# A hybrid decoder block on one core: the split weights of the MLP, the output projection and the branches stand at other places in their buffers from block to block

## Chip, cores and metric

The kernel runs on one core of a Trainium2 chip. The metric is the device time of one execution in microseconds, given as the median of several runs. Lower is better.

## What is computed

The reference is one decoder layer on 256 tokens of width 2048 with 16 learned tokens ahead of them (272 positions). Two mixers run side by side on the normalized input, RWKV-7 and a forgetting attention, are gated and merged, and a SwiGLU MLP of width 5632 follows.

```
proj = rms(h, n1) @ w_in                          # 2048 x 10704
y_a, y_b = rwkv7(...), fox(...)                   # 1024 wide each
g_a, g_b = split(sigmoid(z_gate))
merged = g_a * (y_a @ w_a) + g_b * (y_b @ w_b)    # "branches"
h = h + merged @ w_o                              # "output projection"
gate, up = split(rms(h, n2) @ w_gu)               # MLP, 2 x 5632 columns
return h + (silu(gate) * up) @ w_dn
```

All of it is float32.

## The kernel before

Every large matrix product is done in split precision. A weight block of 128 x 1024 words is loaded by one DMA into a tile `raw` (four buffers). ScalarE (ACT) copies it, rounded, into a tile `wh` (the high part), and VectorE (DVE) writes the remainder `raw - wh` into a tile `wl` (the low part); there are four buffers of each, and a buffer has 1088 words in each partition. The helper `wload` (L304) issues these three steps. Activations are split likewise into a high and a low part that lie next to each other, 272 words each, so the pair of one block of 128 features takes 544 words in each partition. Of the four products of parts three are taken.

Three kinds of block use these weights.

- *MLP, gate and up* (`cm_jobs`, L432, called at L1369 and L1370): 11 blocks of each, named `gt0` to `gt10` and `up0` to `up10`, with 512 columns of the weight each. The weights are the stationary operand (128 x 128), the activation tile `hts` moves. `mm2` (L419) gives one matmul of 512 columns with `wh`, which moves the high and the low part of the activation one after the other (L423), and one of 256 columns with `wl`, which moves the high part (L425; L422 in the last feature block). A block is 16 feature blocks by 4 column groups: 64 such pairs, fed by 8 loads.
- *Branches* (`cm_jobs` from `branch_jobs`, L1259): 16 blocks of 256 weight columns, fed by 2 loads each. `mm3` (L346) gives three matmuls of 256 columns: `wh` with the high part (L347), `wh` with the low part (L348), `wl` with the high part (L349). There are 16 such triples in a block.
- *Output projection and down projection* (`tm_jobs`, L1285; called at L1329 for `wo0` to `wo3` and L1378 for `dn0` to `dn3`): here the activations (`mgh`, `mgl`, `ach`, `acl`) are stationary, and the weights move, 512 columns at a time, as two stretches of 256 words that stand 272 words apart. Three matmuls to a triple: L1304 (high weights, high activation), L1305 (high weights, low activation) and L1306 (low weights, high activation). 32 triples in a `wo` block, 88 in a `dn` block.

In `cm_jobs` the split weights fill the first 1024 words of their buffer, one feature block behind the other, from word 0 on. In `tm_jobs` (`gap=True`) the four stretches of 256 words begin at words 16, 288, 560 and 832:

```
th, tl = (t.rearrange("p (r c) -> p r c", c=L)[:, :, NMETA:] for t in (wh, wl))
```

The order of the work on TensorE (PE) is the program's own. A load is issued ahead of the matmuls of the block that came before it (`run`, L408), so that loading and splitting run beside the matmuls. The gate columns of `w_in` (`zg`), and other columns of `w_in`, use `cm_jobs` as well. All the blocks named above come after the first 613 us of the execution, in the order branches, output projection, gate and up, down projection.

Of the kernel before, what the change touches and what calls it, by code (L numbers as in the profile page):

```python
# [18 lines left out]
P = 128  # L19
D = 2048  # L20
NMETA = 16

T = 256
L = NMETA + T
# [3 lines left out]
DFF = 5632  # L28
# [6 lines left out]
KT = D // P  # L35
# [18 lines left out]
GATEB = 3  # L54
PSM = 4
WCOLS = 4 * L

LANES = 112
BETWEEN = 2
# [41 lines left out]
def hybrid_block(ctx, tc, A, out, dbg=None):  # L101
# [199 lines left out]
        nc.tensor.matmul(pz, zw, zw, start=True, stop=True)  # L301


    def wload(parts, n, between=None, gap=False):  # L304

        raw = wp.tile([P, 1024], F32, tag="raw", name="raw", bufs=RAWB)
        wh = wp.tile([P, WCOLS], F32R, tag="wh", name="wh", bufs=WB)
        wl = wp.tile([P, WCOLS], F32R, tag="wl", name="wl", bufs=WB)  # L310
        if gap:

            (_, _, shape, ((_, src),)), = parts
            nc.sync.dma_start(raw.rearrange("p (k c) -> p k c", c=shape[1]), src)
            rr = raw.rearrange("p (r c) -> p r c", c=T)
            th, tl = (t.rearrange("p (r c) -> p r c", c=L)[:, :, NMETA:] for t in (wh, wl))
            nc.scalar.activation(th, rr, AF.Copy)  # L317
            nc.vector.tensor_tensor(tl, rr, th.bitcast(F32), op=ALU.subtract)  # L318
            return [(th, tl)]
        res = []  # L320
        for prow, c0, shape, srcs in parts:
            size = 1
            for d in shape:
                size *= d
            names = " ".join(f"d{i}" for i in range(len(shape)))
            kw = {f"d{i}": d for i, d in enumerate(shape)}

            def v(t):
                return t[:prow, c0:c0 + size].rearrange(f"p ({names}) -> p {names}", **kw)

            for sel, src in srcs:
                nc.sync.dma_start(v(raw)[sel], src)
            if between is not None:
                between(len(res))
            cs_ = slice(c0, c0 + size)
            nc.scalar.activation(wh[:prow, cs_], raw[:prow, cs_], AF.Copy)  # L336
            nc.vector.tensor_tensor(wl[:prow, cs_], raw[:prow, cs_], wh[:prow, cs_].bitcast(F32), op=ALU.subtract)  # L337
            res.append((v(wh), v(wl)))
        return res
# [3 lines left out]
    def kblock(ap):  # L343
        return ap.rearrange("(k p) c -> p k c", p=P)
# [63 lines left out]
    def run(jobs):  # L408
        for load, mul in jobs:
            w = load()  # L410
            finish_job()
            pending.append(lambda w=w, mul=mul: mul(w))
# [16 lines left out]
        nc.scalar.activation(dst, ps[:, :T], AF.Copy)  # L429
        nc.vector.tensor_tensor(dst, dst, ps[:, T:], op=ALU.add)  # L430

    def cm_jobs(wap, nk, act, n0, n, post, alloc=main_ps, name="cm", two=True):  # L432


        box = []
        cols = wap.shape[1]
        nm, kb = cols // P, 1024 // cols

        def mk(q):
            def load():  # L440
                return wload([(P, 0, [kb, cols], [((ALL,), kblock(wap[q * kb * P:(q + 1) * kb * P, :]))])], 1024)

            def mul(w):
                (wh, wl), = w
                if q == 0:
                    box.extend(alloc(f"{name}_{m}") for m in range(nm))
                for m in range(nm):
                    ms = slice(m * P, (m + 1) * P)
                    for k in range(kb):
                        kt = q * kb + k  # L450
                        a = act[:, kt, :, n0:n0 + n]
                        if n == T and two:
                            mm2(box[m], wh[:, k, ms], wl[:, k, ms], a, kt == 0, kt == nk - 1)
                        else:
                            mm3(box[m][:, :n], wh[:, k, ms], wl[:, k, ms], a[:, 0], a[:, 1], kt == 0, kt == nk - 1)
                        slot(3 * n / 2.4)
                if q == nk // kb - 1:
                    post(box)
            return load, mul
        return [mk(q) for q in range(nk // kb)]  # L460
# [778 lines left out]
    def branch_jobs(j):  # L1239
        tl = gate_tile(j)  # L1240
        for b in range(2):
            if (j, b) in spilled:
                nc.sync.dma_start(tl[:, b], zgd[j, :, b])
        jobs = []

        def post(b):
            def f(pss):
                if b == 0:
                    tf = tl.rearrange("p b m t -> p (b m) t")
                    nc.vector.tensor_tensor(tf, tf, bcast(rsb[:, NMETA:], 4), op=ALU.mult)  # L1250
                    nc.scalar.activation(tl, tl, AF.Sigmoid)
                for m in range(2):
                    nc.vector.tensor_tensor(tl[:, b, m, :], pss[m][:, :T], tl[:, b, m, :], op=ALU.mult)
                if b == 1:
                    nc.vector.tensor_tensor(tl[:, 0], tl[:, 0], tl[:, 1], op=ALU.add)
                    split(mgh[:, 2 * j:2 * j + 2, :], mgl[:, 2 * j:2 * j + 2, :], tl[:, 0])
            return f
        for b, (wn, act) in enumerate((("w_branch_a", yas), ("w_branch_b", ybs))):
            jobs += cm_jobs(A[wn][0][:, j * 256:(j + 1) * 256], 8, act, NMETA, T, post(b),  # L1259
                            alloc=aux_ps, name=f"br{b}{j}", two=False)  # L1260
        return jobs

    ahead = gate_jobs()
# [18 lines left out]
    rs2 = hp.tile([P, 2], F32, tag="rs2", name="rs2")  # L1282
    rsb2 = hp.tile([P, T], F32, tag="rsb2", name="rsb2")

    def tm_jobs(wap, nk, ah, al, post, name):  # L1285

        box = []

        def mk(q):
            def load():  # L1290
                return wload([(P, 0, [2, 512], [((ALL,), kblock(wap[q * 256:(q + 1) * 256, :]))])], 1024, gap=True)

            def mul(w):
                (wh, wl), = w
                if q == 0:
                    box.extend(main_ps(f"{name}_{t}") for t in range(2))
                end = q == nk // 2 - 1
                for k, t in ((0, 0), (1, 0), (0, 1), (1, 1)):
                    kt = q * 2 + k
                    ts_ = slice(t * P, (t + 1) * P)  # L1300
                    first, last = kt == 0, kt == nk - 1
                    o = box[t].rearrange("p (a c) -> p a c", a=2)
                    hi, lo_ = wh[:, 2 * k:2 * k + 2], wl[:, 2 * k:2 * k + 2]
                    nc.tensor.matmul(o, ah[:, kt, ts_], hi, start=first, stop=False)  # L1304
                    nc.tensor.matmul(o, al[:, kt, ts_], hi, start=False, stop=False)  # L1305
                    nc.tensor.matmul(o, ah[:, kt, ts_], lo_, start=False, stop=last)  # L1306
                    if end and k == 1:
                        post(t, box[t])
            return load, mul
        return [mk(q) for q in range(nk // 2)]  # L1310

    for j in range(4):
        js = slice(j * 512, (j + 1) * 512)
        nc.sync.dma_start(hh[:, :, js], x[:, js].rearrange("(t p) c -> p t c", p=P))

        def post(t, ps, j=j, js=js):
            nc.vector.tensor_tensor(hh[:, t, js], ps, hh[:, t, js], op=ALU.add)
            jk = hp.tile([P, 512], F32, tag="jk", name=f"jk{j}{t}", bufs=2)
            nc.scalar.activation(jk, hh[:, t, js], AF.Square, accum_out=ss2[:, t, j:j + 1])
            if t == 0:  # L1320
                return
            for k in range(4 * j, 4 * j + 4):
                pt = aux_ps(f"hT{k}")[:, :T]
                for t in range(2):
                    nc.tensor.transpose(pt[:, t * P:(t + 1) * P], hh[:, t, k * P:(k + 1) * P], ident)
                tmp = hp.tile([P, T], F32, tag="htmp", name=f"htmp{k}", bufs=3)
                nc.vector.tensor_scalar(tmp, pt, vc("n2", k), None, op0=ALU.mult)
                split(hts[:, k, 0, NMETA:], hts[:, k, 1, NMETA:], tmp)
        run(tm_jobs(A["w_o"][0][:, js], KT, mgh, mgl, post, f"wo{j}"))  # L1329
    finish_job()  # L1330
    nc.vector.tensor_reduce(rs2, ss2, axis=AX.X, op=ALU.add)
    ms2 = hp.tile([P, 2], F32, tag="ms2", name="ms2")
# [20 lines left out]
    for j in range(DFF // 512):  # L1353
# [8 lines left out]
        def post_up(pss, gs=gs, j=j):  # L1362
            for m, (g, ps) in enumerate(zip(gs, pss)):
# [2 lines left out]
                nc.vector.tensor_tensor(ub, ub, rsb2, op=ALU.mult)  # L1366
                nc.vector.tensor_tensor(ub, ub, g, op=ALU.mult)
                split(ach[:, 4 * j + m, :], acl[:, 4 * j + m, :], ub)
        run(cm_jobs(wgu[:, j * 512:(j + 1) * 512], KT, hts, NMETA, T, post_gate, name=f"gt{j}"))  # L1369
        run(cm_jobs(wgu[:, DFF + j * 512:DFF + (j + 1) * 512], KT, hts, NMETA, T, post_up, alloc=aux_ps, name=f"up{j}"))  # L1370
    wdn = A["w_down"][0]
    for j in range(4):
        js = slice(j * 512, (j + 1) * 512)

        def post(t, ps, js=js):
            nc.vector.tensor_tensor(hh[:, t, js], ps, hh[:, t, js], op=ALU.add)
            nc.sync.dma_start(out[0][t * P:(t + 1) * P, js], hh[:, t, js])
        run(tm_jobs(wdn[:, js], NF, ach, acl, post, f"dn{j}"))  # L1378
    finish_job()
    hp_pool.__exit__(None, None, None)  # L1380
    ap_pool.__exit__(None, None, None)
# [61 lines left out]
```

## Time and profile before

| | us |
|---|---|
| median of 3 runs | 1537.64 (1537.41 to 1539.07) |
| the profiled execution | 1540.85 |
| its span, first to last instruction | 1539.1 |
| PE busy in the span | 1529.6 (99%) |
| weight loads of PE (PEld) busy | 1352.5 (88%) |
| DVE busy | 1030.4 (67%) |
| ACT busy | 778.2 (51%) |

The page lists, for each engine, the time in which it had an instruction under way. Matmuls overlap: a matmul's listed duration is longer than the time that it holds the array, since the next one starts before it ends. What a matmul costs the kernel is therefore read from the distance between starts. The granted TensorE clock is 0.999 of full speed over the span.

### The profile page before, as it was taken

The numbers are of one execution on the slowest core, as the hardware profiler recorded it, in microseconds if no ns is written. First come the engines' busy times: TensorE is split into PE (matmuls) and PEld (weight loads), VectorE is DVE, ScalarE is ACT, GpSimd is POOL, SyncE is SP. The second block draws the span as 40 slices with busy tenths as digits, with TensorE's granted clock in tenths as the row PEclk, the third lists the DMA queues.
The fourth block names the chain that finished last, engine by engine and source line by source line (L and its number), as shares of the span: only waits on it lengthen the run. The fifth ranks groups of instructions, "written<-read, shape, count | busy, mean of one in ns | idle before, by whom it ended". The sixth has DMA issues, their size and how long they took to land.

```text
span 1539.1 us, 25987 instructions
## 1 busy us (share of the span) xinstructions
PE 1529.6 (99%) x10113; PEld 1352.5 (88%) x10113; DVE 1030.4 (67%) x1859; ACT 778.2 (51%) x1174; POOL 106.8 (7%) x186
## 2 busy tenths in 40 slices
PE   9999999999999999999999999999999999999998
PEld 9999899989989888998888888888888888888887
DVE  7887698688788857876565566666556666444443
ACT  7654465475465445554455455445445544333332
POOL 2111203302202000000000000000000000000000
PEclk9999999999999999999999999999999999999999
DMA  8566546546645757777566666666666665566663
GB/s 269 163 171 185 148 134 188 163 119 188 175 125 154 212 155 218 230 226 240 181 180 185 192 185 186 191 192 182 189 191 191 182 190 189 191 204 204 189 203 104
DMA packets 211483, 283.32 MB, mean 184 GB/s; under 512 B 23888, under 2 KB 128352, under 8 KB 211360
## 3 DMA queue, kind: packets, MB, share of 16 engines
q1 hardware_dynamic: 206752, 277.53, 60.7%
q10 hardware_dynamic: 4608, 4.13, 0.8%
q8 instruction: 79, 1.29, 0.3%
q14 instruction: 44, 0.36, 0.1%
HBM read 274.43 MB, written 7.19 MB: 183 GB/s over the span
## 4 chain that ended last, share of the span: by engine, by line
PE 95%; DVE 2%; ACT 1%; DMA 1%; SPq 1%; issue 1%; DVEq 0%; ACTq 0%
PE up L423 11%; PE gt L423 10%; PE zg L423 8%; PE dn L1306 5%; PE dn L1305 5%; PE dn L1304 5%; PE up L425 5%; PE gt L425 5%; PE zg L425 4%; PE f L347 2%; PE f L349 2%; PE f L348 2%; PE br L347 2%; PE f L423 2%; PE br L348 2%; PE br L349 2%
## 5 line engine op out<-in xcount | busy, mean ns | idle before, releaser
L337 DVE TENSOR_TENSOR wl<-raw,wh 128x1024 fp32r<-128x1024 f32 (+1 forms) x376 | 456.7, 1216 | 264.0 <-ACT wh L336 263.4
L336 ACT ACTIVATE wh<-raw 128x1024 fp32r<-128x1024 f32 (+1 forms) x376 | 393.9, 1049 | 424.8 <-PE up L423 117.5
L318 DVE TENSOR_TENSOR wl<-raw,wh 128x1024 fp32r<-128x1024 f32 x120 | 147.0, 1225 | 162.8 <-ACT wh L317 162.7
L423 PE MATMUL gt<-hts,wh 128*128 128x512 f32 x704 | 245.0, 394 | 0.0
L423 PE MATMUL up<-hts,wh 128*128 128x512 f32 x704 | 244.9, 394 | 0.0
L317 ACT ACTIVATE wh<-raw 128x1024 fp32r<-128x1024 f32 x120 | 127.0, 1058 | 194.4 <-PE dn L1305 141.5
L425 PE MATMUL gt<-hts,wl 128*128 128x256 f32 x660 | 186.2, 282 | 0.0
L425 PE MATMUL up<-hts,wl 128*128 128x256 f32 x660 | 186.0, 282 | 0.0
L423 PE MATMUL zg<-xhl,wh 128*128 128x512 f32 x512 | 182.4, 401 | 0.0
L423 PEld LDWEIGHTS up<-hts,wh 128*128 128x128 f32 x704 | 130.1, 188 | 26.5
L423 PEld LDWEIGHTS gt<-hts,wh 128*128 128x128 f32 x704 | 130.1, 188 | 26.5
L1305 PE MATMUL dn<-wh,acl 128*128 128x512 f32 x352 | 138.7, 394 | 0.0
L1306 PE MATMUL dn<-wl,ach 128*128 128x512 f32 x352 | 138.3, 393 | 0.0
L1304 PE MATMUL dn<-wh,ach 128*128 128x512 f32 x352 | 138.1, 392 | 0.0
L425 PE MATMUL zg<-xhl,wl 128*128 128x256 f32 x480 | 135.0, 281 | 0.0
L425 PEld LDWEIGHTS up<-hts,wl 128*128 128x128 f32 x660 | 124.7, 189 | 1.8
L425 PEld LDWEIGHTS gt<-hts,wl 128*128 128x128 f32 x660 | 124.7, 189 | 1.8
L423 PEld LDWEIGHTS zg<-xhl,wh 128*128 128x128 f32 x512 | 94.3, 188 | 19.4 <-issue 0.7
L425 PEld LDWEIGHTS zg<-xhl,wl 128*128 128x128 f32 x480 | 90.6, 189 | 1.2
L1304 PEld LDWEIGHTS dn<-wh,ach 128*128 128x128 f32 x352 | 66.0, 188 | 15.7
L1305 PEld LDWEIGHTS dn<-wh,acl 128*128 128x128 f32 x352 | 66.1, 188 | 15.4
L1306 PEld LDWEIGHTS dn<-wl,ach 128*128 128x128 f32 x352 | 66.1, 188 | 14.7
(464 smaller groups left out, 2937.9 us busy)
## 6 DMA issues: line engine op xcount, KB each, us to landing
raw<-in_w_gate_up_dram SPq DMA_DIRECT2D x176, 512.0 KB, 3.7
raw<-in_w_in_dram SPq DMA_DIRECT2D x160, 512.0 KB, 4.1
raw<-in_w_down_dram SPq DMA_DIRECT2D x88, 512.0 KB, 4.8
raw<-in_w_o_dram SPq DMA_DIRECT2D x32, 512.0 KB, 4.1
raw<-in_w_branch_a_dram SPq DMA_DIRECT2D x16, 512.0 KB, 4.6
raw<-in_w_branch_b_dram SPq DMA_DIRECT2D x16, 512.0 KB, 4.7
zgd<-zg ACTq DMA_DIRECT2D x30, 128.0 KB, 1.7
gate<-zgd SPq DMA_DIRECT2D x15, 256.0 KB, 6.0
```

The lines of the kernel that those rows point to most:

```text
L317: nc.scalar.activation(th, rr, AF.Copy)
L318: nc.vector.tensor_tensor(tl, rr, th.bitcast(F32), op=ALU.subtract)
L336: nc.scalar.activation(wh[:prow, cs_], raw[:prow, cs_], AF.Copy)
L337: nc.vector.tensor_tensor(wl[:prow, cs_], raw[:prow, cs_], wh[:prow, cs_].bitcast(F32), op=ALU.subtract)
L347: nc.tensor.matmul(ps, wh, ah, start=first, stop=False)
L348: nc.tensor.matmul(ps, wh, al, start=False, stop=False)
L349: nc.tensor.matmul(ps, wl, ah, start=False, stop=last)
L423: nc.tensor.matmul(ps.rearrange("p (a t) -> p a t", a=2), wh, act, start=first, stop=last)
L425: nc.tensor.matmul(ps[:, :T], wl, act[:, 0, :], start=False, stop=False)
L1304: nc.tensor.matmul(o, ah[:, kt, ts_], hi, start=first, stop=False)
L1305: nc.tensor.matmul(o, al[:, kt, ts_], hi, start=False, stop=False)
L1306: nc.tensor.matmul(o, ah[:, kt, ts_], lo_, start=False, stop=last)
```

## The change

Nothing is taken out of the work and nothing is added. `wload` gets a parameter `lay` in place of `gap`, and places its two output tiles by it. Three tables give the places: `PLACES` for the 22 blocks of gate and up, `PLACES_T` for the four blocks of the output projection and the four of the down projection, `PLACES_BR` for the 16 branch blocks. An entry of `PLACES` or `PLACES_BR` is (odd, first word of `wh`, first word of `wl`).

- odd = 0: the 1024 words begin at the given word (0, 8, 16 or 24) in place of word 0.
- odd = 1: even feature blocks stand in the first 544 words of the buffer and odd ones in the second 544, each from the given word on (0 to 32), so that an odd feature block is 544 words behind the even one in place of 512.
- `tm_jobs` has pairs: the four stretches of 256 words begin 0, 8 or 16 words into their 272, for high and low part apart, where it was 16 for both.

`cm_jobs` without an entry (the columns of `w_in`) takes (0, 0, 0). For blocks of 256 columns the four feature blocks of a load now lie in the order 0, 2, 1, 3, so there ScalarE and VectorE read `raw` as four stretches of 256 words. The list of instructions of the built program, with its waits, is the same as before on each engine, but for the shape of the split's output in blocks with odd = 1, which is 128x2x512 in place of 128x1024.

```diff
+PLACES = [(0, a, b) for a in (0, 8, 16, 24) for b in (0, 8, 16, 24)][1:] + [
+    (1, 24, 24), (1, 8, 8), (1, 16, 16), (1, 8, 24), (1, 24, 8), (1, 16, 0), (1, 0, 16)]
+PLACES_T = [(8, 0), (0, 8), (16, 8), (8, 16), (0, 0), (8, 8), (16, 0), (0, 16)]
+PLACES_BR = [(0, 8, 8), (0, 16, 16), (0, 24, 24), (0, 0, 8), (0, 0, 16), (0, 0, 24), (0, 8, 0), (0, 16, 0),
+             (1, 0, 0), (1, 8, 8), (1, 16, 16), (1, 24, 24), (1, 32, 0), (1, 32, 8), (1, 32, 16), (1, 32, 24)]
...
-    def wload(parts, n, between=None, gap=False):
+    def wload(parts, n, between=None, lay=None):
...
-        if gap:
+        if lay is not None:
             (_, _, shape, ((_, src),)), = parts
+            odd, *first = lay
             nc.sync.dma_start(raw.rearrange("p (k c) -> p k c", c=shape[1]), src)
-            rr = raw.rearrange("p (r c) -> p r c", c=T)
-            th, tl = (t.rearrange("p (r c) -> p r c", c=L)[:, :, NMETA:] for t in (wh, wl))
+            if odd is None:
+                rr = raw.rearrange("p (r c) -> p r c", c=T)
+                th, tl = (t.rearrange("p (r c) -> p r c", c=L)[:, :, s:s + T] for t, s in zip((wh, wl), first))
+            else:
+                rr = raw.rearrange("p (j q c) -> p q j c", q=2, c=shape[1])
+                th, tl = ((t if odd else t[:, s:s + 1024]).rearrange("p (q e) -> p q e", q=2)
+                          [:, :, odd and s:(odd and s) + 512].rearrange("p q (j c) -> p q j c", c=shape[1])
+                          for t, s in zip((wh, wl), first))
             nc.scalar.activation(th, rr, AF.Copy)
             nc.vector.tensor_tensor(tl, rr, th.bitcast(F32), op=ALU.subtract)
...
-                            mm2(box[m], wh[:, k, ms], wl[:, k, ms], a, kt == 0, kt == nk - 1)
+                            mm2(box[m], wh[:, k % 2, k // 2, ms], wl[:, k % 2, k // 2, ms], a, kt == 0, kt == nk - 1)
...
-                            alloc=aux_ps, name=f"br{b}{j}", two=False)
+                            alloc=aux_ps, name=f"br{b}{j}", two=False, lay=PLACES_BR[2 * j + b])
...
-        run(tm_jobs(A["w_o"][0][:, js], KT, mgh, mgl, post, f"wo{j}"))
+        run(tm_jobs(A["w_o"][0][:, js], KT, mgh, mgl, post, f"wo{j}", PLACES_T[j]))
...
-        run(cm_jobs(wgu[:, j * 512:(j + 1) * 512], KT, hts, NMETA, T, post_gate, name=f"gt{j}"))
-        run(cm_jobs(wgu[:, DFF + j * 512:DFF + (j + 1) * 512], KT, hts, NMETA, T, post_up, alloc=aux_ps, name=f"up{j}"))
+        run(cm_jobs(wgu[:, j * 512:(j + 1) * 512], KT, hts, NMETA, T, post_gate, name=f"gt{j}",
+                    lay=PLACES[j]))
+        run(cm_jobs(wgu[:, DFF + j * 512:DFF + (j + 1) * 512], KT, hts, NMETA, T, post_up, alloc=aux_ps, name=f"up{j}",
+                    lay=PLACES[11 + j]))
...
-        run(tm_jobs(wdn[:, js], NF, ach, acl, post, f"dn{j}"))
+        run(tm_jobs(wdn[:, js], NF, ach, acl, post, f"dn{j}", PLACES_T[4 + j]))
```

## Rows read from the trace of the kernel before

**Rows 1.** Busy time by stretch: us, then each engine's busy time, clock, DMA, GB/s.
```profile
0.00:620.00 620.00, 614.47 (x5108) 562.28 (x5109) 497.17 (x1156) 354.14 (x628) 106.77 (x186) 1.00 0.60 173
620.00:713.00 93.00, 93.00 (x752) 91.51 (x751) 68.56 (x88) 46.83 (x49) 0.00 (x0) 1.00 0.69 218
713.00:803.00 90.00, 90.00 (x414) 73.11 (x413) 54.60 (x72) 43.78 (x63) 0.00 (x0) 1.00 0.66 206
803.00:1291.00 488.00, 487.87 (x2789) 427.65 (x2788) 295.89 (x438) 241.41 (x345) 0.00 (x0) 1.00 0.65 188
1291.00:1539.00 248.00, 244.22 (x1057) 197.99 (x1055) 114.17 (x108) 92.00 (x91) 0.00 (x0) 1.00 0.57 183
```

**Rows 2.** The page's chain that ended last: share of the span by engine.
```profile
PE 95%; DVE 2%; ACT 1%; DMA 1%; SPq 1%; issue 1%; DVEq 0%; ACTq 0%
```

**Rows 3.** Timeline of PE around the start of `up5` and of `gt6`: start, duration, what.
```profile
1044.61 0.39 PE L423 MATMUL up<-hts,wh 128*128 128x512 f32 x1
1044.84 0.28 PE L425 MATMUL up<-hts,wl 128*128 128x256 f32 x1
1044.95 0.40 PE L423 MATMUL up<-hts,wh 128*128 128x512 f32 x1
...
1067.01 0.39 PE L423 MATMUL gt<-hts,wh 128*128 128x512 f32 x1
```

**Rows 4.** PE groups by line: count, busy time, mean duration of one.
```profile
L423 PE MATMUL gt<-hts,wh 128*128 128x512 f32 x704 | 245.0, 394 | 0.0
L425 PE MATMUL gt<-hts,wl 128*128 128x256 f32 x660 | 186.2, 282 | 0.0
L1305 PE MATMUL dn<-wh,acl 128*128 128x512 f32 x352 | 138.7, 394 | 0.0
L1306 PE MATMUL dn<-wl,ach 128*128 128x512 f32 x352 | 138.3, 393 | 0.0
L1304 PE MATMUL dn<-wh,ach 128*128 128x512 f32 x352 | 138.1, 392 | 0.0
```

**Rows 5.** Tile `up`, 1050 to 1060 us: durations, minimum/median/maximum, in ns.
```profile
L425 PE MATMUL up<-hts,wl x30: 281/282/283, 1049.7 to 1059.9; 128*128 128x256 f32 x30
L423 PE MATMUL up<-hts,wh x29: 393/396/396, 1049.9 to 1059.7; 128*128 128x512 f32 x29
```

**Rows 6.** Tile `br`, whole span: durations as above.
```profile
L347 PE MATMUL br<-yas,wh x128: 279/282/285, 613.7 to 699.0; 128*128 128x256 f32 x128
...
L349 PE MATMUL br<-yas,wl x128: 280/280/281, 614.0 to 699.2; 128*128 128x256 f32 x128
L347 PE MATMUL br<-ybs,wh x128: 282/284/285, 619.4 to 704.7; 128*128 128x256 f32 x128
...
L348 PE MATMUL br<-ybs,wh x128: 279/280/282, 619.5 to 704.8; 128*128 128x256 f32 x128
```

**Rows 7.** Tile `dn`, 1352 to 1413 us (block `dn1`): durations as above.
```profile
L1306 PE MATMUL dn<-wl,ach x89: 392/394/394, 1351.8 to 1412.8; 128*128 128x512 f32 x89
L1304 PE MATMUL dn<-wh,ach x88: 392/392/393, 1352.0 to 1412.3; 128*128 128x512 f32 x88
...
L1305 PE MATMUL dn<-wh,acl x88: 392/394/396, 1352.3 to 1412.6; 128*128 128x512 f32 x88
```

**Rows 8.** The page's groups of the splits: busy, mean ns | idle before, releaser.
```profile
L337 DVE TENSOR_TENSOR wl<-raw,wh 128x1024 fp32r<-128x1024 f32 (+1 forms) x376 | 456.7, 1216 | 264.0 <-ACT wh L336 263.4
L336 ACT ACTIVATE wh<-raw 128x1024 fp32r<-128x1024 f32 (+1 forms) x376 | 393.9, 1049 | 424.8 <-PE up L423 117.5
L318 DVE TENSOR_TENSOR wl<-raw,wh 128x1024 fp32r<-128x1024 f32 x120 | 147.0, 1225 | 162.8 <-ACT wh L317 162.7
...
L317 ACT ACTIVATE wh<-raw 128x1024 fp32r<-128x1024 f32 x120 | 127.0, 1058 | 194.4 <-PE dn L1305 141.5
```

**Rows 9.** Chain that ended last, 803 to 900 us: start, us, what.
```profile
803.39 1.07 ACT wh L336
804.48 1.23 DVE wl L337
```

**Rows 10.** PE groups by line: the output projection and one branch line.
```profile
L1306 PE MATMUL wo<-wl,mgh 128*128 128x512 f32 x128 | 50.6, 396 | 0.0
L1305 PE MATMUL wo<-wh,mgl 128*128 128x512 f32 x128 | 50.6, 395 | 0.0
L1304 PE MATMUL wo<-wh,mgh 128*128 128x512 f32 x128 | 50.3, 393 | 0.0
...
L347 PE MATMUL br<-ybs,wh 128*128 128x256 f32 x128 | 36.3, 284 | 0.0
L347 PE MATMUL br<-yas,wh 128*128 128x256 f32 x128 | 36.3, 283 | 0.0
```

More of the change, by code (lines that the diff above doesn't have):

```diff
@@ L430, in halves, with cm_jobs @@
         nc.vector.tensor_tensor(dst, dst, ps[:, T:], op=ALU.add)
-    def cm_jobs(wap, nk, act, n0, n, post, alloc=main_ps, name="cm", two=True):
+    def cm_jobs(wap, nk, act, n0, n, post, alloc=main_ps, name="cm", two=True, lay=(0, 0, 0)):
         box = []
@@ L440, in load @@
             def load():
-                return wload([(P, 0, [kb, cols], [((ALL,), kblock(wap[q * kb * P:(q + 1) * kb * P, :]))])], 1024)
+                return wload([(P, 0, [kb, cols], [((ALL,), kblock(wap[q * kb * P:(q + 1) * kb * P, :]))])], 1024,
+                             lay=lay)
             def mul(w):
@@ L452, in mul @@
                         if n == T and two:
-                            mm2(box[m], wh[:, k, ms], wl[:, k, ms], a, kt == 0, kt == nk - 1)
+                            mm2(box[m], wh[:, k % 2, k // 2, ms], wl[:, k % 2, k // 2, ms], a, kt == 0, kt == nk - 1)
                         else:
-                            mm3(box[m][:, :n], wh[:, k, ms], wl[:, k, ms], a[:, 0], a[:, 1], kt == 0, kt == nk - 1)
+                            mm3(box[m][:, :n], wh[:, k % 2, k // 2, ms], wl[:, k % 2, k // 2, ms], a[:, 0], a[:, 1],
+                                kt == 0, kt == nk - 1)
                         slot(3 * n / 2.4)
@@ L1283, in hybrid_block, with tm_jobs @@
     rsb2 = hp.tile([P, T], F32, tag="rsb2", name="rsb2")
-    def tm_jobs(wap, nk, ah, al, post, name):
+    def tm_jobs(wap, nk, ah, al, post, name, lay=(NMETA, NMETA)):
         box = []
@@ L1290, in load @@
             def load():
-                return wload([(P, 0, [2, 512], [((ALL,), kblock(wap[q * 256:(q + 1) * 256, :]))])], 1024, gap=True)
+                return wload([(P, 0, [2, 512], [((ALL,), kblock(wap[q * 256:(q + 1) * 256, :]))])], 1024,
+                             lay=(None, *lay))
             def mul(w):
```

## The prediction

> **What bounds the kernel now.** I read the stretches first. From 620 us on, PE is busy without a break: 93.00 of 93.00 us in the branches, 90.00 of 90.00 in the output projection, 487.87 of 488.00 in gate and up, at a granted clock of 1.00, which is the 2.4 GHz level [rows 1]. DVE has 295.89 us of work in the 488 and ACT 241.41, so both splitting engines rest four tenths of the time or more. The chain of work that ended last says the same: 95% of it lies on PE [rows 2]. So only what a matmul takes counts, and then how long one holds the array. A busy engine does not say that; the distance between starts does.
>
> Block `up5` starts at 1044.61 us and `gt6` at 1067.01 [rows 3]. That is 22.40 us for 64 pairs, 350.0 ns to a pair of 512 and 256 columns. At 2.4 GHz 768 columns would take 320 ns. So about 30 ns of each pair, over 8%, is something other than columns. Within a pair, the 512 columns hold the array for about 0.23 us and the 256 for about 0.11 to 0.12 [rows 3]. Their mean durations are 394 and 282 ns, together 676 [rows 4]; against 350 that leaves 163 ns for each matmul that overlaps the next. I therefore read a duration less 163 ns as the time held: 231 for the 512, 119 for the 256.
>
> This gives a fine scale, for durations are listed to the nanosecond, and they are not all equal. In ten microseconds of `up` the 512-column matmuls take 393 or 396 ns, the 256-column ones 281 to 283 [rows 5]. In the branches the same kind takes 279 to 285 [rows 6]. In `dn1` L1304 takes 392 or 393 and L1305 392 to 396 [rows 7]. Column count, engine clock and instruction are the same within each row. What changes from one matmul to the next within a line is the address: the activation pair of the next feature block stands 544 words further on, the weights 512 words or, in the down projection, 544. So I take it that **the place of the operands matters, by up to about 6 ns in 119 and 4 in 231**. Which relation of the two places is good the rows do not say.
>
> **The change, part by part.** Loads, splits and matmuls keep their number and their order, so nothing is removed or added on any queue, and no wait is new. Three things remain.
>
> *The splits.* ACT and DVE write shifted or two-part outputs, and in blocks of 256 columns they read four stretches. The nearest row is the split that already writes four stretches of 256 words: 1058 ns on ACT and 1225 on DVE, against 1049 and 1216 for the plain one (a mean that has a few smaller ones in it) [rows 8]. So about 9 ns on each. In gate and up a load's 8 pairs hold PE for 2.8 us, and one split costs DVE 1.23 and ACT 1.07: hidden, and it stays so until a split grows by a microsecond. ACT waits for PE there to free a buffer (117.5 us behind `up` L423), not PE for ACT [rows 8]. Where the cover is gone, as at the first load of the MLP, one split of each kind stands on the chain [rows 9], and the price is 18 ns at a place; a dozen such places make 0.2 us. If all 160 loads of `w_in` stood bare it would be 160 x 18 ns = 2.9 us, but PE is busy 614.47 of the first 620 us [rows 1]. I take 0.
>
> *The columns of `w_in`* get their feature blocks in another order, moved by 256 words. The `up` rows, where weight blocks are 128, 512 and 1088 words apart in four buffers, show only the two alternating values, 393 and 396, so such steps do not show. I take 0.
>
> *The places in 5024 matmuls.* 22 blocks x 64 = 1408 pairs in gate and up, 480 triples in the output and down projections (1440 matmuls), 256 triples in the branches (768).
>
> The trace of before does not show the new places, so I bound them by the shortest and longest durations of a matmul of that width at the places that it does show: 392 and 396 for 512 columns [rows 7], 279 and 285 for 256 [rows 6].
>
> - Gate and up now 394 + 282 = 676 [rows 4]. All at the short ends: 671, -5 ns x 1408 = -7.0 us. All at the long ends: 681, +7.0 us.
> - Projections: 1056 at (392 + 394 + 393)/3 = 393.0 [rows 4] and 384 at (393 + 395 + 396)/3 = 394.7 [rows 10], mean 393.4. Short -1.4 x 1440 = -2.0 us, long +2.6 x 1440 = +3.7 us.
> - Branches: L347 at 283 and 284 [rows 10], the other two lines at 280 [rows 6], mean 281.2. Short -2.2 x 768 = -1.7 us, long +3.8 x 768 = +2.9 us.
>
> Together -10.7 to +13.6 us, if every new place were the best or the worst of those seen. The tables spread over many places, so an average over relations is the nearer guess. I take for each kind the mean of its own value and that of the other kind of the same width. For 512 columns that is between 394 and 393.4, for 256 between 282 and 281.2. Gate and up: (-0.3 - 0.4) x 1408 = -1.0 us. Projections: +0.3 x 1440 = +0.4. Branches: +0.4 x 768 = +0.3. **Sum: -0.3 us.**
>
> The profiled execution took 1540.85 us with a span of 1539.1, 3.2 us above the median of the runs. A difference of blocks carries over to the median as it is: 1537.64 - 0.3 = 1537.3 us. About 0.2% or 3.1 us is what a measurement of this kernel can tell from no change. Over 5024 matmuls that is **0.61 ns each**, so a small shift of the mean already decides.
>
> **The rivals.**
>
> *Some places make the stall go away.* Of a pair's 350 ns, 30 are not columns [rows 3]. If a place had nothing of that, a block of 64 pairs would win 1.9 us, and two such blocks of 22 would show as faster; four give -7.7 us, about 1530. Halfway, with the mean at half the short bounds (-5.3 us), it is 1532.3. For it: the stall is large and depends on place. Against: none of the relations shown, with stationary and moving weights, goes below 279 and 392 ns, which is 116 and 229 held.
>
> The Trainium skill bears on this, in TensorE: Matmul & The Clock Gate, section Back-to-back issue gap: matmuls in isolation follow each other at columns over 2.4 GHz plus 2.5 ns, about 216 ns at 512. The 231 held here is not that. By that rule a place without stall would be worth about 25 ns to a pair.
>
> *Place means nothing for stationary weights.* The 393 and 396 could come from the moving address alone. Then gate, up and branches stay as they are and only the 1440 matmuls of the projections can move, by -2.0 to +3.7 us: about 1537.6, not to be told from no change. For it: in rows 5 every alternation can be put to `hts`. Against: in the branches, L347 and L349 move the same words of `yas`, and one takes 279 to 285 where the other takes 280 or 281 [rows 6]. What differs is the weights that are fetched beside them. I give this a fifth, inside the chance of no change.
>
> The Trainium skill goes further, in SBUF — State Buffer, section Who interferes with whom: TensorE has two independent read ports, one for the moving operand and one for weights, and waits on nobody. By it the change is worth 0 and no block differs from another; the spread in rows 5 and 6 speaks against a rule that has no room for place.
>
> *Slower: weight fetch and moving operand meet more often in gate and up.* Before, `wh` and `wl` start alike, so both fetches meet the moving operand in the same two ways. In 16 of the 22 blocks, and in six of the eight of the projections, high and low part now start apart, relations that no row shows, and the long values (396, 285) are further from the means than the short ones in projections and branches. If the mean moves half way to the long ends, that is +6.8 us: 1544.4. It decides from 0.61 ns a matmul on, if spread over all; on gate and up alone from 3.1 us / 1408 = 2.2 ns a pair, 352.2 in place of 350.0. For it: the bounds reach further up than down. Against: pairs in two relations already average near the middle of the ends, (671 + 681)/2 = 676.
>
> **How the numbers follow.** The forecast, a mean shift under 0.61 ns either way (with the rival that place means little), has 0.58. Slower by the meeting of the streams 0.22, faster by good places 0.20. The range takes in half of both bounds, 1537.6 - 5.3 = 1532.3 and 1537.6 + 6.8 = 1544.4. The outer halves, where nearly all blocks would have to be at one end, are left out, with some 0.15.
>
> **What would show it.** In the profile after, block starts tell each place: blocks of gate and up should lie between 64 x 345 ns = 22.1 us and 64 x 355 = 22.7 us, some above and some below the 22.40 of now, with a mean within 0.14 us of it. Durations should stay within 279 to 285 and 392 to 396, but no longer alternate alike in all blocks. Splits should stay near 1.06 and 1.23 us, and PE busy near 99%. All blocks at 22.40 would mean that place is nothing beside stationary weights. A block under 22 us would show the stall going away, and the forecast would be wrong on the fast side; a mean over 22.54 us would show the streams meeting, and it would be wrong on the slow side.

## The result, and the profile after

The changed kernel takes 1542.08 us (median of 15 runs) against 1538.04 for the kernel before on the same chip (15 runs): a ratio of 1.0023 with a 95% interval of 1.0016 to 1.0030, about +3.5 us (2.5 to 4.6). The kernel became slower. The loss is clear of zero, but it is hardly larger than the 3.1 us up to which the prediction speaks of no change.

The profiled execution alone would not show it: it took 1540.79 us with a span of 1539.1, as long as that of before. The timeline of PE tells where the time went. Here are the starts of the first branch block, of `gt0` and of the blocks of the down projection, `dn0` and `dn1` before the change, then `dn0` to `dn3` after it (columns: start, duration, what).

```profile
613.72 0.28 PE L347 MATMUL br<-yas,wh 128*128 128x256 f32 x1
...
796.78 0.40 PE L423 MATMUL gt<-hts,wh 128*128 128x512 f32 x1
...
1291.01 0.39 PE L1304 MATMUL dn<-wh,ach 128*128 128x512 f32 x1
...
1352.02 0.39 PE L1304 MATMUL dn<-wh,ach 128*128 128x512 f32 x1
```

```profile
610.52 0.28 PE L361 MATMUL br<-yas,wh 128*128 128x256 f32 x1
...
793.13 0.39 PE L437 MATMUL gt<-hts,wh 128*128 128x512 f32 x1
...
1288.37 0.39 PE L1321 MATMUL dn<-wh,ach 128*128 128x512 f32 x1
...
1349.67 0.40 PE L1321 MATMUL dn<-wh,ach 128*128 128x512 f32 x1
...
1412.11 0.39 PE L1321 MATMUL dn<-wh,ach 128*128 128x512 f32 x1
...
1473.41 0.39 PE L1321 MATMUL dn<-wh,ach 128*128 128x512 f32 x1
```

Branches and output projection: 183.06 us before, 182.61 after. Gate and up: 494.23 and 495.24. From `dn0` to the end of the span: 248.1 and 250.7. That is -0.45, +1.0 and +2.6, together **+3.1 us**. The part before the branches took 3.2 us less in this one execution, which hides the loss. In the profiles of the experiments that part ends between 610.5 and 613.2 us whatever the places are, so the blocks have to be compared, not the spans.

In the changed kernel's rows of the down projection the starts are 61.30, 62.44 and 61.30 us apart, where a block of before takes 61.01. The block with its weights at (8, 8), `dn1`, holds over half of the 2.6 us. Its tile's rows (durations, minimum/median/maximum):

```profile
L1323 PE MATMUL dn<-wl,ach x89: 394/395/403, 1349.4 to 1411.9; 128*128 128x512 f32 x89
...
L1321 PE MATMUL dn<-wh,ach x88: 390/399/400, 1349.7 to 1411.4; 128*128 128x512 f32 x88
...
L1322 PE MATMUL dn<-wh,acl x88: 387/396/403, 1349.9 to 1411.6; 128*128 128x512 f32 x88
```

Against 392 to 396 before [rows 7], the long ones now reach 403.

The splits stayed hidden. Their groups on the changed kernel's page answer to [rows 8]:

```profile
L332 DVE TENSOR_TENSOR wl<-raw,wh 128x1024 fp32r<-128x1024 f32 x488 | 598.3, 1227 | 428.7 <-ACT wh L331 427.9
L331 ACT ACTIVATE wh<-raw 128x1024 fp32r<-128x1024 f32 x488 | 516.7, 1059 | 620.2 <-PE dn L1322 143.9
```

1227 and 1059 ns, and ACT still waits for PE.

The table has the blocks, from their starts in the timeline. `gt0`, in which PE waits, is left out: it takes 23.83 before and after. All is in us; a branch block takes 5.71 before, from 5.62 to 5.75 after.

| blocks | before | after, with (odd, wh, wl) or (wh, wl) |
|---|---|---|
| gate and up, shortest | 22.40 | 22.21 (0,24,8); 22.22 (0,8,16); 22.22 (0,16,24) |
| most | 22.40 | 22.37 to 22.47 |
| longest | 22.40 | 22.58 (0,24,16), (0,8,0); 22.61 (0,8,8); 22.67 (1,8,24); 22.74 (1,24,8), (1,16,0) |
| `wo1`, `wo2`, `wo3` | 23.18 | 23.18 (0,8); 23.07 (16,8); 23.07 (8,16) |
| `dn0` to `dn3` | 61.01 | 61.31 (0,0); 62.44 (8,8); 61.30 (16,0); 61.59 (0,16) |

### The profile page after: what moved, and what is told of

Its sections match the earlier page's. It is cut to its first block, busy times and chain, and to the rows that moved or that the text cites. A ratio compares the mean times of both kernels' runs of the same rounds, so it can differ in the third digit from the quotient of the medians.

```text
span 1539.1 us, 25987 instructions
## 1 busy us (share of the span) xinstructions
PE 1531.0 (99%) x10113; PEld 1351.4 (88%) x10113; DVE 1031.1 (67%) x1859; ACT 778.6 (51%) x1174; POOL 107.4 (7%) x186
## 4 chain that ended last, share of the span: by engine, by line
PE 95%; DVE 2%; ACT 1%; DMA 1%; SPq 1%; issue 1%; DVEq 0%; ACTq 0%
PE up L437 11%; PE gt L437 10%; PE zg L437 8%; PE dn L1322 5%; PE dn L1323 5%; PE dn L1321 5%; PE up L439 5%; PE gt L439 5%; PE zg L439 4%; PE f L361 2%; PE f L363 2%; PE f L362 2%; PE br L363 2%; PE br L361 2%; PE f L437 2%; PE br L362 2%
## 5 line engine op out<-in xcount | busy, mean ns | idle before, releaser
L332 DVE TENSOR_TENSOR wl<-raw,wh 128x1024 fp32r<-128x1024 f32 x488 | 598.3, 1227 | 428.7 <-ACT wh L331 427.9
L331 ACT ACTIVATE wh<-raw 128x1024 fp32r<-128x1024 f32 x488 | 516.7, 1059 | 620.2 <-PE dn L1322 143.9
L361 PE MATMUL f<-xhl,wh 128*128 128x272 f32 x256 | 76.6, 299 | 0.0
L363 PE MATMUL f<-xhl,wl 128*128 128x272 f32 x256 | 73.7, 288 | 0.0
```

Of the source, the lines that this page charges most:

```text
L361: nc.tensor.matmul(ps, wh, ah, start=first, stop=False)
L363: nc.tensor.matmul(ps, wl, ah, start=False, stop=last)
```

## Experiments

Three theories were put against each other. **A**: a block's time follows from its own places. **B**: the loss comes from the splits, or from the part before the branches. **C**: the same places can have more than one steady pace, and what ran ahead of a block decides which.

### Parts of the change, alone and undone

```diff
 e1_projections_back
-PLACES_T = [(8, 0), (0, 8), (16, 8), (8, 16), (0, 0), (8, 8), (16, 0), (0, 16)]
+PLACES_T = [(16, 16)] * 8
 e2_projections_alone
+PLACES = [(0, 0, 0)] * 22
+PLACES_BR = [(0, 0, 0)] * 16
 e3_old_places
+PLACES = [(0, 0, 0)] * 22
+PLACES_BR = [(0, 0, 0)] * 16
+PLACES_T = [(16, 16)] * 8
```

> The changed kernel with the output and down projections back at their old places (16, 16); gate, up and branches keep the new ones. Theory A (each block's time follows from its own places; the profile after has gate and up 1.0 us longer, branches 0.4 shorter, output projection 0.1 shorter, down projection 2.6 longer): +0.6 us on the kernel before, about 1538.6, dn blocks at 61.0 us again. Theory B (the loss comes from the splits, which write and read in more stretches, or from the part before the branches): still +3.5 us, about 1541.5.

Measured: ratio 1.0010 (1.0001 to 1.0018); 1539.02 us against 1538.75. All four `dn` blocks are at 61.01 us. By its blocks, branches to gate and up, the profile is 0.7 us longer than that of before.

> The new places in the output and down projections alone; gate, up and branches at (0, 0, 0). Theory A: +2.5 us on the kernel before, about 1540.5, with dn1 at 62.4 us and gate and up blocks at 22.40. Theory B: as in the run with all places old, 0 if the splits of gate and up are to blame.

Measured: 1.0025 (1.0014 to 1.0036); 1541.46 us. `dn1` is at 62.44, every block of gate and up but the first at 22.40. The starts of `dn1` and `dn2`:

```profile
1349.22 0.40 PE L1322 MATMUL dn<-wh,ach 128*128 128x512 f32 x1
...
1411.66 0.39 PE L1322 MATMUL dn<-wh,ach 128*128 128x512 f32 x1
```

> The changed kernel with every place as it was before; what is left of the change is the order of the feature blocks of w_in and the branches in their buffer, with the splits that read four stretches. Theory A: no difference to the kernel before, 0 within 1 us. Theory B (the splits cost): up to 160 x 18 ns = +2.9 us, all of it before the branches.

Measured: 1.0000 (0.9991 to 1.0009); 1538.53 us. All blocks have the times of before.

What follows: B is out. With the new order of feature blocks and the splits in more stretches, but the old places, nothing is lost, to within 0.1%. The places in the projections alone bring most of the loss, as A has it; gate, up and branches together come to little.

### The places that looked good, in all blocks

```diff
 e4_good_places
+PLACES = [(0, 24, 8)] * 22
+PLACES_BR = [(1, 8, 8)] * 16
+PLACES_T = [(8, 16)] * 8
```

> All blocks of a kind at one place that was short in the profile after: gate and up (0, 24, 8), branches (1, 8, 8), projections (8, 16). Theory A: 22 x -0.19 - 16 x 0.09 - 4 x 0.12 - 4 x 0.33 (the last from 0.12 us of a wo block by 88/32 triples) = -7.4 us, about 1530.6, gate and up blocks all at 22.2. Theory C (a block's time in that profile hung on its position or its neighbours and not on its own place): blocks of one kind differ though their places are the same, and the sum is within 1 us of the kernel before.

Measured: 1.0037 (1.0024 to 1.0049); 1543.80 us, 5 to 6 us slower where A forecast -7.4 us. Branches and projections did as expected: 16 branch blocks at 5.60 us, four `dn` blocks at 60.72. But every block of gate and up after the first takes **22.80 us**, not 22.2. First come the starts of `up1` and `gt2` in the timeline, then the durations in `up1`, and last the durations of the same stretch in the changed kernel, where `up1` has the same places:

```profile
861.05 0.40 PE L438 MATMUL up<-hts,wh 128*128 128x512 f32 x1
...
883.85 0.40 PE L438 MATMUL gt<-hts,wh 128*128 128x512 f32 x1
```

```profile
L438 PE MATMUL up<-hts,wh x57: 396/398/404, 861.8 to 881.7; 128*128 128x512 f32 x57
L440 PE MATMUL up<-hts,wl x56: 282/285/287, 862.0 to 882.0; 128*128 128x256 f32 x56
```

```profile
L437 PE MATMUL up<-hts,wh x59: 390/391/397, 861.7 to 881.9; 128*128 128x512 f32 x59
...
L439 PE MATMUL up<-hts,wl x57: 279/280/281, 862.0 to 881.4; 128*128 128x256 f32 x57
```

The same instructions on the same addresses are listed 5 to 7 ns longer each, throughout the block. A alone cannot say that. Nor did C come true as it is worded ahead of this run, for the blocks do not differ from each other and the sum is not that of before.

The first gate block of this run, `gt0`, shows both paces at one place. In the rows below a feature block of four pairs starts at each row of L438. The row with `prb` is a break: PE waits for the norm of the MLP and makes two transposes for it.

```profile
797.87 0.39 PE L438 MATMUL gt<-hts,wh 128*128 128x512 f32 x1
...
799.26 0.39 PE L438 MATMUL gt<-hts,wh 128*128 128x512 f32 x1
...
800.65 0.39 PE L438 MATMUL gt<-hts,wh 128*128 128x512 f32 x1
801.21 0.41 PE L1357 MATMUL prb<-ident,ob 128*128 128x128 f32 x2 [0.17 <-DVE ob L1356]
...
802.63 0.40 PE L438 MATMUL gt<-hts,wh 128*128 128x512 f32 x1
...
804.06 0.40 PE L438 MATMUL gt<-hts,wh 128*128 128x512 f32 x1
```

Four pairs take 1.39 us ahead of the break and 1.43 us behind it, and the slow pace then stays.

### Repeats, to see whether the block ahead matters

```diff
 e5_repeats (gate and up, in the order of execution, wh and wl, odd = 0)
+(0,0) (24,8) (24,8) (0,16) (24,8) (24,8) (24,8) (8,16) (8,16) (8,16) (16,24)
+(16,24) (16,24) (0,0) (0,0) (8,16) (8,16) (24,8) (24,8) (16,24) (16,24) (0,0)
+PLACES_BR = [(1, 8, 8)] * 16
+PLACES_T = [(8, 8), (8, 8), (16, 16), (8, 8), (8, 8), (8, 8), (8, 16), (8, 8)]
```

> Gate and up in the order of execution: (0,0); (24,8) twice; (0,16); (24,8) three times; (8,16) three times; (16,24) three times; (0,0) twice; (8,16) twice; (24,8) twice; (16,24) twice; (0,0). Projections wo0 and wo1 (8,8), wo2 (16,16), wo3 (8,8), dn0 and dn1 (8,8), dn2 (8,16), dn3 (8,8). Branches (1,8,8). Theory C (a place has more than one steady pace, and a block keeps the one into which the blocks ahead of it brought PE): blocks with the same places differ, (24,8) at 22.2 in some and 22.8 in others, and a block that follows its like keeps its time. Theory A (place alone): equal places give equal times everywhere; the run with (24,8) in all blocks then has to differ from the changed kernel by something else than its history, and (24,8) is 22.8 here in all five-odd places. Down projection (8,8) by A and by C: 62.4, (8,16) 60.7.

Starts of `up0` to `gt3` in its timeline; from `up0` on the places are (24,8), (24,8), (0,16), (24,8), (24,8):

```profile
818.22 0.39 PE L438 MATMUL up<-hts,wh 128*128 128x512 f32 x1
...
840.43 0.40 PE L438 MATMUL gt<-hts,wh 128*128 128x512 f32 x1
...
863.23 0.39 PE L438 MATMUL up<-hts,wh 128*128 128x512 f32 x1
...
885.62 0.39 PE L438 MATMUL gt<-hts,wh 128*128 128x512 f32 x1
...
907.83 0.40 PE L438 MATMUL up<-hts,wh 128*128 128x512 f32 x1
...
930.63 0.40 PE L438 MATMUL gt<-hts,wh 128*128 128x512 f32 x1
```

The blocks take 22.21, 22.80, 22.39, 22.21 and 22.80 us. A block at (24,8) behind (0,0), (0,16) or (8,16) took 22.2 (three of three), one behind its like 22.8 (four of four), with gate and up blocks in both lots. So C holds, but not as it was worded: a block at (24,8) does not keep the pace of a quick one of its like, it falls to the slow one behind it. The places (8,16) and (16,24) took 22.20 to 22.23 in all ten blocks, behind their like too. In the down projection (8,8) took 62.4 to 62.5 in its three blocks, also directly behind gate and up: its loss belongs to the place, as far as these runs show. The kernel took 1541.70 us in its one run, beside 1538.60 for before.

### Distance or address

```diff
 e6_all_shifted
-    hts = hp.tile([P, KT, 2, L], F32R, tag="hts", name="hts")
+    hts = hp.tile([P, KT * 2 * L + 64], F32R, tag="hts", name="hts")
+    hts = hts[:, 8:8 + KT * 2 * L].rearrange("p (k s t) -> p k s t", s=2, t=L)
...
+    ach = ach[:, 56:56 + NF * T].rearrange("p (k t) -> p k t", t=T)
+    acl = acl[:, 56:56 + NF * T].rearrange("p (k t) -> p k t", t=T)
+PLACES: each wh and wl + 8; the last four of PLACES_T: (0, 0), (0, 0), (8, 8), (0, 8)
```

> The changed kernel with the activations of gate and up (hts) 8 words further on and every place of gate and up 8 words further on too; in the down projection the stationary activations (ach, acl) 56 words further on and the weights at (0,0), (0,0), (8,8), (0,8). If only the distance of the two operands counts (modulo 64 words): gate and up as in the changed kernel, block by block (up1 22.21, up8 22.74, up9 22.74), dn0 and dn1 as (8,8) before them, 62.4, dn2 as (16,16), 61.0, dn3 as (8,16), 60.7. If the place of the moving operand or of the weights alone counts: other times, gate and up as if at the places of the table plus 8, dn0 and dn1 at 61.3.

Every block of gate and up has its time of the changed kernel within 0.01 us. The starts of `up1` and `gt2`, then of the four `dn` blocks:

```profile
862.18 0.39 PE L438 MATMUL up<-hts,wh 128*128 128x512 f32 x1
...
884.40 0.39 PE L438 MATMUL gt<-hts,wh 128*128 128x512 f32 x1
...
1288.80 0.39 PE L1323 MATMUL dn<-wh,ach 128*128 128x512 f32 x1
...
1351.20 0.40 PE L1323 MATMUL dn<-wh,ach 128*128 128x512 f32 x1
...
1413.68 0.39 PE L1323 MATMUL dn<-wh,ach 128*128 128x512 f32 x1
...
1474.70 0.39 PE L1323 MATMUL dn<-wh,ach 128*128 128x512 f32 x1
```

`up1` takes 22.22, as at (0,24,8) with `hts` unmoved. The two `dn` blocks at (0,0) take 62.40 and 62.48, the time of (8,8), where (0,0) with unmoved activations takes 61.31. The one at (8,8) takes 61.02, the time of (16,16), and the last, at (0,8), 60.7, the time of (8,16). So **what counts is the distance between the moving operand and the stationary one**, not the address of either. In the down projection distances that differ by 64 words gave the same time: weights at 0 with the activations moved by 56 words take the time of weights at 8 with the activations unmoved. The run took 1541.20 us beside 1538.60.

One block does not fit a theory of place and block ahead alone. `wo1` has in this run the places of the changed kernel, behind a `wo0` that has them too, and the shift touches neither operand of the output projection; yet it takes 23.48 us in place of 23.18. Early in it the triples are broken by transposes of the residual (`hT`). Here are the rows of one line of `wo1` behind that break, in the changed kernel and in this run:

```profile
L1323 PE MATMUL wo<-wl,mgh x26: 392/392/393, 728.0 to 745.4; 128*128 128x512 f32 x26
```

```profile
L1325 PE MATMUL wo<-wl,mgh x26: 399/400/401, 728.2 to 745.8; 128*128 128x512 f32 x26
```

So blocks of the output projection have more than one pace as well, and here the places of the block ahead are not what chose it.

### Steady places everywhere, and more places

```diff
 e7_steady_places
+PLACES = [(0, 16, 24)] * 22
+PLACES_BR = [(1, 8, 8)] * 16
+PLACES_T = [(8, 16)] * 8
```

> All of gate and up at (16,24), which stayed at 22.2 us in the run with repeats also behind its like; branches (1,8,8), projections (8,16). Theory C (place and the pace at entry): 22 blocks at 22.2 (-4.2 us), branches -1.7, output projection -0.4, down projection -1.2: -7.5 us on the kernel before, about 1531. Theory D (a block at a good place only is quick behind a block at another place): gate and up go to 22.8 as with (24,8) in all blocks, +8.8 -3.3, about 1544.

Measured: **0.9949 (0.9936 to 0.9963); 1530.53 us** against 1537.96, a version that beats both kernels. Every block of gate and up after the first is at 22.20, so theory D does not hold for this place. Here are the starts of `up5` and `gt6`, to be read beside [rows 3]:

```profile
1037.16 0.39 PE L438 MATMUL up<-hts,wh 128*128 128x512 f32 x1
...
1059.37 0.39 PE L438 MATMUL gt<-hts,wh 128*128 128x512 f32 x1
```

The pair costs 346.9 ns in place of 350.0. Branches 89.60 us (91.30 before), output projection 91.34 (91.76), down projection blocks 60.72 (61.01).

> Gate and up by two blocks at each place, in the order of execution: (0,8), (24,32), (0,32), (0,40), (0,48), (0,56), (8,48), (16,56), (24,56), (8,32), (16,40); branches by two at (1,24,24), (1,0,8), (1,8,16), (1,16,24), (0,16,0), (0,8,16), (0,16,24), (1,8,0); down projection (16,8), (0,8), (8,0), (8,16). Theory C: every block between 22.1 and 22.9 us; a place's second block shows its pace behind its like, and at some places it differs from the first. Theory A: first and second block are always equal. By scaling the output projection, down (16,8) is 60.7.

```diff
 e8_more_places (gate and up, in the order of execution, two blocks each, odd = 0)
+(0,8) (24,32) (0,32) (0,40) (0,48) (0,56) (8,48) (16,56) (24,56) (8,32) (16,40)
+PLACES_T = [(8, 16)] * 4 + [(16, 8), (0, 8), (8, 0), (8, 16)]
```

One run of 1537.01 us beside 1537.96. No place of gate and up beats (16,24): 22.76 and 22.74 at (24,32), 22.20 and then 22.38 at (0,40), between 22.37 and 22.47 at the rest. So (0,40) is a second place whose block behind its like is slower than the first. The branches stood at eight places, two blocks each, and took 5.60 to 5.71, none better than (1,8,8). Down (16,8) took 60.75, as expected. The down projection had here the four places that the output projection has in the changed kernel, and from `dn0` to the end of the span it took 247.9 us, 0.2 less than before. This is the row of that stretch: its ends, its length and the busy times of the engines, PE first.

```profile
1287.37:1535.27 247.90, 243.98 (x1057) 197.93 (x1055) 114.16 (x108) 92.25 (x91) 0.00 (x0) 1.00 0.60 183
```

## Why the prediction was wrong

**What held.** PE alone is the bound; the distance between starts is the cost. The splits at 0 and the new order of `w_in` at 0: the run with the old places has a ratio of 1.0000. Place matters beside stationary weights too: the blocks of gate and up range from 22.21 to 22.74. The rival that only the moving address counts falls with that, for `hts` stands still in all 22 blocks; and in the shifted run `hts` moved together with the weights and no block changed. The Trainium skill, in SBUF — State Buffer, section Who interferes with whom, gives TensorE two independent read ports, one for the moving operand and one for weight loads, and says that it never waits on anyone. Taken to mean that place cannot matter, it does not fit these blocks: moving the weights alone changed their times. Whether a port is what makes a matmul longer no run shows. The time lies inside the range. The signs that the prediction gave for gate and up came out nearly as written: blocks of 22.21 to 22.74 us behind `gt0` where it has 22.1 to 22.7, with a mean of 22.45, within 0.14 of 22.40. For the projections, where the loss fell, it gave the durations alone as a sign, and these left their bounds.

**What failed** is the step "I take for each kind the mean of its own value and that of the other kind of the same width", which gave -0.3 us and with it no change as the likeliest. Its terms against the blocks of the profile: gate and up -1.0, measured +1.0; branches +0.3, measured -0.3; projections +0.4, measured **+2.4** (output -0.1, down +2.6). The last is the term that decided. The step took places as exchangeable draws from the few relations shown. They are not: one pair of places, (8,8), makes a triple of the down projection 62.44 / 88 = 709.5 ns in place of 693.3, and with 88 triples to a block that one of eight table entries weighs 1.4 us. The other three `dn` blocks are 0.3 to 0.6 us slower than before, and the good entries, (16,8) and (8,16), stand in the output projection, where a block has 32 triples. Which half of the table fell to the large blocks was chance: in the run with more places the down projection has the output projection's four entries, and it took 0.2 us less than before in place of 2.6 more.

(8,8) even passes the bound: three matmuls at the long end, 396 less 163, would be 699 ns. So the longest duration at the places shown was no bound for places not shown, and neither was 355 ns a pair, since the 22.80 us of the run with (24,8) everywhere is 356. Nor were 392 and 396 the ends of what the trace of before shows. In `wo1`, behind its break, it has 512-column matmuls of 388 and of 398 ns:

```profile
L1304 PE MATMUL wo<-wh,mgh x31: 388/394/398, 728.9 to 749.7; 128*128 128x512 f32 x31
```

So "none of the relations shown, with stationary and moving weights, goes below 279 and 392 ns" is a misreading. The wider ends would not have saved the bound: three at 398 are 705 ns.

The rest was closeness: +3.1 us over 5024 matmuls is 0.62 ns each, where the prediction's own line was 0.61 ns.

**The rival that was slower** had the direction and the size at which it decides, but not the place. It looked to gate and up and to blocks whose high and low part start apart. Of those, (16,8) and (8,16) are the best in the projections and (16,24) is the best in gate and up; the worst block of the projections has both alike, while the two worst of gate and up have them apart. So standing apart decides nothing by itself. **The faster rival** was right that good places exist, but no run shows that the stall can go: the best pair found, 346.9 ns, still has 27 beyond its columns.

What stays open is why some distances are bad, and what picks the pace when a stream of matmuls starts or goes on behind a break. The runs show that both exist; no run shows the mechanism.

## What to carry to other kernels

Where PE is the bound, the distance between the moving operand and the stationary one inside their buffers was worth up to 2% of a block either way here; give a table of places to the blocks of one kernel and read each block's time from the distance of starts in one profile. Then run the winner in *all* blocks before believing it: a place can be quick behind another and slow behind its like, as (24,8) was. And where a few large blocks stand beside many small ones, weigh each table entry by the matmuls that it governs.

## What the runs showed of the hardware

A stream of matmuls with the same addresses can have more than one steady pace: 22.2 or 22.8 us for the same block of 64 pairs at (24,8). The pace changed within a block where other matmuls came between, from 1.39 to 1.43 us for four pairs. And the cost goes by the distance of the two operands: moving both operands of gate and up by 8 words left every block's time as it was within 0.01 us.
